# A two-layer encoder trunk on one core: down operands split in place and spread over more products, running sums copied by ScalarE, all down products of layer 0 in chunks, S5 preparation begun beside w_out

## The chip, the cores and the metric

The kernel runs on one core of a Trainium2 chip. The metric is the device time of one execution in microseconds; a kernel's time is the median of its runs.

## The reference

Two pre-norm residual layers over 1024 tokens of width 1024, in float32. Each layer has a token mixer (an S5 state-space branch and a windowed attention branch, gated and summed, then `w_out`) and a SwiGLU feed-forward of width 2816; a final RMSNorm closes. What the change touches is the feed-forward, and the S5 parameters that are prepared beside it:

```python
for layer in range(DEPTH):                      # 2
    hn = rmsnorm(h, norm1_g[layer])
    ...
    h = h + merged @ w_out[layer]
    hn2 = rmsnorm(h, norm2_g[layer])
    ff = jax.nn.silu(hn2 @ ffn_w_gate[layer]) * (hn2 @ ffn_w_up[layer])
    h = h + ff @ ffn_w_down[layer]
```

## The kernel before

All operands are float32, and every product is made of three matmuls of rounded parts (type fp32r): high by high, high by low, low by high. A value is split into parts by a ScalarE cast (the high part) and a VectorE subtraction (the low part); `split` (L113 to L117) does it for activations, L157, L158, L169 and L170 for weights. One matmul multiplies a 128x128 weight tile by a 128x512 operand into one PSUM bank, so the token axis has two halves. `chain` (L181 to L183) makes a whole sum over the contraction in one bank, `piece` (L192 to L194) a part of one.

**The feed-forward** (`ffn_items`, from L1178) has 22 tiles `f` of 128 columns for gate and up. The first `QUAD_FROM` of them (8 on layer 0, 3 on layer 1) are plain: four chains of 24 matmuls. The others are quads: one 2x2 block product by Strassen and Winograd's scheme, gate and up being the two rows and the halves of the tokens the two columns, in seven products of 12 matmuls, 84 instead of 96. A quad's products go into banks x, y, v, w; the sums between them (`first`, `second`, `third`, `gate1`, `half0`: L1400 to L1430) are taken out of PSUM: one ScalarE copy of x, and five VectorE additions per quad. tanh (ScalarE, `ts<-qx`, `ts<-qu`) and two fused VectorE operations per half make the SwiGLU.

**The down products.** On layer 0 the first eight tiles of the feed-forward are multiplied plainly in two groups of four (`GROUPS`); everything else goes in chunks (`CHUNKS`) of eight or six tiles. A chunk's operand is a 2x2 block matrix; seven operand sets (b11, b21, b22 and the sums t0 to t3, formed by VectorE in `row`) are stored to DRAM by POOL's queue (`put`), loaded again by SP's queue (`op_load`, L1225: four tiles of 256 KB a set, tiles `fr`) and split (`op_split`, tiles `foh` and `fol`). `down_quad` then makes two rows of output tiles in seven products again: 16 down quads in all, 33 gate quads. The results of a chunk are added to `hs` in DRAM by accumulating stores on POOL's queue; the last chunk adds into the residual directly, half of it plainly (`last_down`).

**What sets the order.** The program is a list of items; an engine's instructions stand in the order of that list as the tile scheduler then arranges them. `do` counts the products of all quads. `at(t, ...)` hangs work behind product t: for a chunk that begins at product t0, set k is loaded at t0−12+1.7k and split at t0−4+k. `mix` spreads side work over a stretch of items: the operand sums of the first quads over the last 12 plain items, the S5 preparation of layer 1 over the plain items of layer 0. Activation tiles of all kinds share 86 SBUF slots of 128x512 (L44, L107); PSUM has 8 banks; raw weights have four buffers and split weights three, which are fetched and split ahead of their products.

Of the kernel before, what the change touches and what calls it, by code (L numbers as in the profile page):

```python
# [8 lines left out]
F32 = mybir.dt.float32  # L9
F32R = mybir.dt.float32r  # L10
# [15 lines left out]
GROUPS = (((0, 4), (4, 4)), ())  # L26
CHUNKS = (((8, 8), (16, 6)), ((0, 8), (8, 8), (16, 6)))
QUAD_FROM = (8, 3)
DOWN_QUADS = 2
SETS = ("b11", "t1", "t0", "b21", "t2", "t3", "b22")  # L30
# [68 lines left out]
class Trunk:  # L99
# [85 lines left out]
    def piece(self, ps, g, off, xs, start):  # L185

        from functools import partial
        mm = partial(self.nc.tensor.matmul, skip_group_check=not start)
        for k, (xh, xl) in enumerate(xs):
            s = off + k * P  # L190
            wh, wl = g.hi[:, s:s + P], g.lo[:, s:s + P]
            mm(ps, lhsT=wh, rhs=xh, start=start and k == 0, stop=False)  # L192
            mm(ps, lhsT=wh, rhs=xl, start=False, stop=False)  # L193
            mm(ps, lhsT=wl, rhs=xh, start=False, stop=k == len(xs) - 1)  # L194

# [982 lines left out]
    def ffn_items(self, l, fill, head):  # L1178
# [43 lines left out]
        def op_load(c, kind):  # L1222
            ts = ops[c, kind] = [self.A("fr") for _ in range(chunks[c][1] // 2)]
            for j, t in enumerate(ts):
                nc.sync.dma_start(t, fd[c, kind, j])  # L1225

        def op_split(c, kind):
            ops[c, kind] = [self.split(t, "fo") for t in ops[c, kind]]
# [69 lines left out]
        def down_quad(c, m):  # L1298
# [7 lines left out]
            def product(bank, g, off, kind, start):  # L1306
                def run():
                    if start:
# [4 lines left out]
            p = [product(*a) for a in (("x", q.a, 0, "b11", True), ("y", q.b, w, "t1", True), ("v", q.b, 0, "t0", True),  # L1313
                                       ("x", q.a, w, "b21", False), ("y", q.c, 0, "t2", False), ("w", q.d, 0, "t3", True),
                                       ("v", q.e, 0, "b22", False))]
# [7 lines left out]
            def first():  # L1323
                b["p1"] = self.A("qp")
                nc.scalar.copy(b["p1"], b["x"])

            def second():
                b["u2"] = self.A("qu")
                V.tensor_tensor(b["u2"], b["p1"], b["y"], ADD)
# [9 lines left out]
            def third():  # L1339
                V.tensor_tensor(b["p1"], b["p1"], b["y"], ADD)  # L1340
                b["c22"] = self.A("qc")
                V.tensor_tensor(b["c22"], b["p1"], b["v"], ADD)
                out(1, 1, b["c22"])

            def c21():
                V.tensor_tensor(b["p1"], b["p1"], b["w"], ADD)
                out(1, 0, b["p1"])

            def c12():
                V.tensor_tensor(b["u2"], b["u2"], b["v"], ADD)  # L1350
                out(0, 1, b["u2"])
# [28 lines left out]
        def quad_items(f):  # L1380
# [4 lines left out]
            def product(bank, g, off, xs, start):  # L1385
                def run():
# [6 lines left out]
            p = [product("x", q.a, 0, B(0, 0), True), product("y", q.b, HC, lambda: T[1], True),  # L1393
                 product("v", q.b, 0, lambda: T[0], True), product("x", q.a, HC, B(0, 4), False),
                 product("y", q.c, 0, lambda: T[2], False), product("w", q.d, 0, lambda: T[3], True),
                 product("v", q.e, 0, B(1, 4), False)]

            def first():
                b["p1"] = self.A("qp")
                nc.scalar.copy(b["p1"], b["x"])  # L1400

            def second():
                b["u2"] = self.A("qu")
                V.tensor_tensor(b["u2"], b["p1"], b["y"], ADD)
# [5 lines left out]
            def third():  # L1410
                V.tensor_tensor(b["p1"], b["p1"], b["y"], ADD)
                b["c22"] = self.A("qc")
                V.tensor_tensor(b["c22"], b["p1"], b["v"], ADD)

            def half0():
                s = b["s0"]
                V.scalar_tensor_tensor(s, s, 1.0, b["x"], ADD, MUL)
                V.tensor_tensor(b["p1"], b["p1"], b["w"], ADD)
                V.scalar_tensor_tensor(s, b["p1"], 0.5, s, MUL, MUL)  # L1419
                keep(f, 0, s)  # L1420

            def gate1():
                V.tensor_tensor(b["u2"], b["u2"], b["v"], ADD)  # L1423
                b["s1"] = self.A("ts")
                nc.scalar.activation(b["s1"], b["u2"], AF.Tanh, scale=0.5)  # L1425

            def half1():
# [4 lines left out]
                row(f)  # L1432
# [24 lines left out]
        for i, (G, go, U, uo) in enumerate(blocks):  # L1457
# [17 lines left out]
            if i == quads - 1:  # L1475
                w = 12
# [12 lines left out]
        def at(t, fn):  # L1489
            more.setdefault(t, []).append((fn,))  # L1490

        for t0, c in begins:
            for k, kind in enumerate(SETS):
                at(t0 - 12 + k * 17 // 10, lambda c=c, kind=kind: op_load(c, kind))
                at(t0 - 4 + k, lambda c=c, kind=kind: op_split(c, kind))
# [24 lines left out]
        for i, (p, e) in enumerate(made):  # L1520
            do(p[1])
            main.append(e[0])
            do(p[2])
            main.append(e[1])
            do(p[3])
            do(p[4])
            main.append(e[2])
            do(p[5])
            main.append(e[3])
# [3 lines left out]
            main.append(e[4])  # L1533
            do(p[6])
            main.extend(e[5:])
# [9 lines left out]
    def build(self):  # L1545
# [31 lines left out]
        for l in range(DEPTH):  # L1577
# [89 lines left out]
            ffn = self.ffn_items(l, self.s5_prep_items(1) if l == 0 else None, self.w_out_items(l))  # L1667
# [138 lines left out]
```

## Time and profile before

| | |
|---|---|
| median of 3 runs | 2648.95 us (2644.98 to 2649.70) |
| profiled execution, its own time | 2647.83 us |
| its span | 2646.1 us, granted clock 0.986 on the mean |
| TensorE busy | 2564.8 us, 97% |
| VectorE busy | 1827.9 us, 69% |
| ScalarE busy | 1022.1 us, 39% |
| DMA | 357.01 MB, 135 GB/s on the mean |

The profile is of one execution. PE is the engine that multiplies; "idle before, releaser" tells what an engine waited for. The granted clock is the share of full speed at which the throttle let TensorE run. Matmuls overlap in a pipeline: one takes 0.39 us, the next one starts some 0.23 us after it, so the time of a stretch follows from its count of matmuls. The feed-forward of layer 0 ends in the three hundred us from 1186, that of layer 1 in those from 2376.

### The profile page before, as it was taken

To read this page: it belongs to the slowest core of one execution; us is meant where nothing else is said; L and a number is where in the kernel's file an instruction comes from. 1 tells how busy PE (TensorE), PEld (TensorE's weight loads), DVE (VectorE), ACT (ScalarE), POOL (GpSimd) and SP (SyncE) were. 2 spreads that over 40 slices of the span, in tenths; PEclk is the share of its full clock that TensorE was granted. 3 is DMA by queue.
4 is the path that set the end of the run, shared out by engine and by line. 5 is a ranking of instruction groups with operands and counts; after the bars stand their busy time and mean duration, and the time that the engine had idled before them with its cause. 6 is when DMAs were issued, how large, how long until landed. Compare 5 with 4: busy or idle time off the path is not lost.

```text
span 2646.1 us, 35134 instructions
## 1 busy us (share of the span) xinstructions
PE 2564.8 (97%) x12722; PEld 2088.1 (79%) x12722; DVE 1827.9 (69%) x3577; ACT 1022.1 (39%) x1949; POOL 321.3 (12%) x528
## 2 busy tenths in 40 slices
PE   8999899999999999998999999999999999998997
PEld 6787677887888888886787778888878888886776
DVE  9986878575977677677763465756377777676766
ACT  5336744422443333233444553453233222234432
POOL 0141011000142111011100001200001011111110
PEclk9999999999999999998999999999999999998998
DMA  3453435354174533255732244434322233255773
GB/s 139 136 186 118 136 120 180 124 186 140 55 197 132 98 110 108 96 202 137 200 133 76 72 140 161 159 120 167 127 92 93 102 104 116 92 199 156 176 190 123
DMA packets 160510, 357.01 MB, mean 135 GB/s; under 512 B 22048, under 2 KB 44832, under 8 KB 160336
## 3 DMA queue, kind: packets, MB, share of 16 engines
q1 hardware_dynamic: 117136, 236.28, 26.9%
q0 software_dynamic: 43200, 118.48, 15.9%
q8 instruction: 100, 1.64, 0.2%
q14 instruction: 74, 0.61, 0.1%
HBM read 230.97 MB, written 123.68 MB: 134 GB/s over the span
## 4 chain that ended last, share of the span: by engine, by line
PE 88%; DVE 7%; ACT 2%; issue 1%; DMA 1%; SPq 0%; DVEq 0%; ACTq 0%
PE pj L181 6%; PE pj L182 6%; PE pj L183 6%; PE qx L192 3%; PE qx L193 3%; PE qx L194 3%; PE qy L192 3%; PE qy L194 3%; PE qy L193 3%; PE qv L192 3%; PE qv L193 3%; PE qv L194 3%; PE wo L181 2%; PE wo L183 2%; PE wo L182 2%; PE br L181 2%
## 5 line engine op out<-in xcount | busy, mean ns | idle before, releaser
L181 PE MATMUL pj<-rah,whi 128*128 128x512 f32 x768 | 306.2, 399 | 0.4 <-DVE sm L804 0.4
L182 PE MATMUL pj<-ral,whi 128*128 128x512 f32 x768 | 300.1, 391 | 0.7 <-DVE ral L116 0.7
L183 PE MATMUL pj<-rah,wlo 128*128 128x512 f32 x768 | 299.9, 391 | 0.0
L170 DVE TENSOR_TENSOR wlo<-raw,whi 128x1024 fp32r<-128x1024 f32 (+1 forms) x126 | 145.7, 1156 | 168.3 <-ACT whi L169 159.0
L169 ACT CAST whi<-raw 128x1024 fp32r<-128x1024 f32 (+1 forms) x126 | 125.3, 995 | 273.9 <-PE pj L182 115.1
L181 PEld LDWEIGHTS pj<-rah,whi 128*128 128x128 f32 x768 | 144.7, 188 | 35.4 <-issue 4.7
L182 PEld LDWEIGHTS pj<-ral,whi 128*128 128x128 f32 x768 | 144.8, 189 | 30.9 <-DVE ral L116 2.6
L183 PEld LDWEIGHTS pj<-rah,wlo 128*128 128x128 f32 x768 | 144.5, 188 | 30.8
L1425 ACT ACTIVATE ts<-qu 128x512 f32<-128x512 f32 x33 | 20.9, 633 | 287.2 <-DVE qu L1423 287.2
L804 DVE CUSTOM_DVE_ANT_0 x<-s,bias,nsink 128x384 f32<-128x384 f32 (+1 forms) x128 | 67.5, 581 | 64.0 <-PE s L798 63.9
L1423 DVE TENSOR_TENSOR qu<-qu,qv 128x512 f32<-128x512 f32 x33 | 22.7, 687 | 125.8 <-PE qv L194 125.8
L192 PE MATMUL qx<-rfh,whi 128*128 128x512 f32 x264 | 102.7, 389 | 0.0
L193 PE MATMUL qx<-rfl,whi 128*128 128x512 f32 x264 | 102.7, 389 | 0.0
L194 PE MATMUL qx<-rfh,wlo 128*128 128x512 f32 x264 | 102.7, 389 | 0.0
L976 ACT COPY s5sg<-s5s 64x256 f32<-64x256 f32 x128 | 51.7, 404 | 128.8 <-DVE s5s L971 127.4
L181 PE MATMUL wo<-mgh,whi 128*128 128x512 f32 x256 | 100.0, 391 | 0.0
L1196 POOL DMA_DIRECT2D fd_b<-ts x60 | 32.6, 543 | 553.4 <-DVE ts L1419 464.2
L183 PE MATMUL wo<-mgh,wlo 128*128 128x512 f32 x256 | 99.7, 389 | 0.0
L182 PE MATMUL wo<-mgl,whi 128*128 128x512 f32 x256 | 99.6, 389 | 0.0
L157 ACT CAST whs<-s 128x512 fp32r<-128x512 f32 (+1 forms) x98 | 59.9, 612 | 99.3 <-DVE s L150 93.3
L157 ACT CAST whi<-sm 128x1024 fp32r<-128x1024 f32 (+1 forms) x49 | 50.6, 1033 | 122.7 <-PE qv L193 102.9
L158 DVE TENSOR_TENSOR wlo<-sm,whi 128x1024 fp32r<-128x1024 f32 (+1 forms) x49 | 58.9, 1202 | 41.8 <-ACT whi L157 41.7
(468 smaller groups left out, 7191.0 us busy)
## 6 DMA issues: line engine op xcount, KB each, us to landing
raw<-in_w_in SPq DMA_DIRECT2D x52, 512.0 KB
raw<-in_w_gate SPq DMA_DIRECT2D x44, 512.0 KB
raw<-in_w_up SPq DMA_DIRECT2D x44, 512.0 KB
fd_t<-ft POOLq DMA_DIRECT2D x72, 256.0 KB, 2.7
fr<-fd_t SPq DMA_DIRECT2D x72, 256.0 KB
g<-th POOLq DMA_DIRECT2D x64, 256.0 KB, 2.8
thr<-g SPq DMA_DIRECT2D x64, 256.0 KB
fd_b<-ts POOLq DMA_DIRECT2D x60, 256.0 KB, 2.3
```

Of the source, the lines that this page charges most:

```text
L157: nc.scalar.copy(g.hi[:, n], src)
L158: V.tensor_tensor(g.lo[:, n], src, g.hi[:, n].bitcast(F32), SUB)
L169: nc.scalar.copy(g.hi[:, :n], g.raw[:, :n])
L170: nc.vector.tensor_tensor(g.lo[:, :n], g.raw[:, :n], g.hi[:, :n].bitcast(F32), SUB)
L181: mm(ps, lhsT=wh, rhs=xh, start=k == 0, stop=False)
L182: mm(ps, lhsT=wh, rhs=xl, start=False, stop=False)
L183: mm(ps, lhsT=wl, rhs=xh, start=False, stop=k == n - 1)
L192: mm(ps, lhsT=wh, rhs=xh, start=start and k == 0, stop=False)
L193: mm(ps, lhsT=wh, rhs=xl, start=False, stop=False)
L194: mm(ps, lhsT=wl, rhs=xh, start=False, stop=k == len(xs) - 1)
L804: V.tensor_tensor_reduce(out=x[:, :n], in0=ps[:, :n], in1=self.bias[hd][:, bo:bo + n], op0=ADD, op1=ALU.min, scale=-1.0, scalar=self.nsink ...
L976: nc.scalar.copy(SG[64 * r:64 * r + 64, g * 256:(g + 1) * 256].rearrange("p (d n) -> p d n", d=2), Sv[64 * g:64 * g + 64, :, r])
```

## The change

1. Layer 0 has no plain down groups: its chunks are (0,8), (8,8) and (16,6), as on layer 1. One tile more is plain there (`QUAD_FROM` 9), and the sums for the first quads are spread over 20 plain items instead of 12. So 32 gate quads and 20 down quads are left.
2. Operands are loaded into the tile that will hold the low part and split in place: two slots per operand instead of three. The sets come in another order, with loads and splits at times from two tables.
3. `carry`: ScalarE copies the running sum from one PSUM bank to the next (y from x, z and w from y), and the next product adds onto the copy. VectorE is left with two additions per quad (`qc` and `qu`).
4. The first part of the S5 preparation of layer 1 is mixed into the first ten items of `w_out` of layer 0.

The diff, with lines of context left out:

```diff
...
 DEPTH = 2
 NPAIR = 16
 NFF = 22
-GROUPS = (((0, 4), (4, 4)), ())
-CHUNKS = (((8, 8), (16, 6)), ((0, 8), (8, 8), (16, 6)))
-QUAD_FROM = (8, 3)
+GROUPS = ((), ())
+CHUNKS = (((0, 8), (8, 8), (16, 6)), ((0, 8), (8, 8), (16, 6)))
+QUAD_FROM = (9, 3)
+PREP_BEFORE = 40
 DOWN_QUADS = 2
-SETS = ("b11", "t1", "t0", "b21", "t2", "t3", "b22")
+SETS = ("b11", "t0", "t1", "b21", "t2", "b22", "t3")
+LOADS = (-14, -10, -8, -7, -5, -4, -2)
+SPLITS = (-10, -6, -4, -2, 0, 2, 3)
 QUAD_LOOK = 5
 NEG = -1e30
 EPS = 1e-6
...
+    def carry(self, b):
+        nc, V = self.nc, self.nc.vector
+        def first():
+            b["y"] = self.PS("qy")
+            nc.scalar.copy(b["y"], b["x"])
+        def second():
+            b["z"] = self.PS("qz")
+            nc.scalar.copy(b["z"], b["y"])
+            b["sv"] = self.A("qp")
+            nc.scalar.copy(b["sv"], b["v"])
+        def third():
+            b["w"] = self.PS("qw")
+            nc.scalar.copy(b["w"], b["y"])
+            b["c22"] = self.A("qc")
+            V.tensor_tensor(b["c22"], b["sv"], b["y"], ADD)
+        return first, second, third
...
         def op_load(c, kind):
-            ts = ops[c, kind] = [self.A("fr") for _ in range(chunks[c][1] // 2)]
+            ts = ops[c, kind] = [self.A("fol", F32R) for _ in range(chunks[c][1] // 2)]
             for j, t in enumerate(ts):
-                nc.sync.dma_start(t, fd[c, kind, j])
+                nc.sync.dma_start(t.bitcast(F32), fd[c, kind, j])
         def op_split(c, kind):
-            ops[c, kind] = [self.split(t, "fo") for t in ops[c, kind]]
+            pairs = []
+            for lo in ops[c, kind]:
+                hi = self.A("foh", F32R)
+                nc.scalar.copy(hi, lo.bitcast(F32))
+                V.tensor_tensor(lo, lo.bitcast(F32), hi.bitcast(F32), SUB)
+                pairs.append((hi, lo))
+            ops[c, kind] = pairs
...
-            p = [product(*a) for a in (("x", q.a, 0, "b11", True), ("y", q.b, w, "t1", True), ("v", q.b, 0, "t0", True),
-                                       ("x", q.a, w, "b21", False), ("y", q.c, 0, "t2", False), ("w", q.d, 0, "t3", True),
-                                       ("v", q.e, 0, "b22", False))]
+            p = [product(*a) for a in (("x", q.a, 0, "b11", True), ("v", q.b, 0, "t0", True), ("y", q.b, w, "t1", False),
+                                       ("x", q.a, w, "b21", False), ("y", q.c, 0, "t2", False), ("z", q.e, 0, "b22", False),
+                                       ("w", q.d, 0, "t3", False))]
             def out(i, h, x):
                 if at_end:
...
                 else:
                     nc.gpsimd.dma_start(self.hs[m + i, h], x, accum_op=ADD)
-            def first():
-                b["p1"] = self.A("qp")
-                nc.scalar.copy(b["p1"], b["x"])
-            def second():
-                b["u2"] = self.A("qu")
-                V.tensor_tensor(b["u2"], b["p1"], b["y"], ADD)
+            first, second, carry = self.carry(b)
             def c11():
                 if at_end:
...
                 out(0, 0, t)
             def third():
-                V.tensor_tensor(b["p1"], b["p1"], b["y"], ADD)
-                b["c22"] = self.A("qc")
-                V.tensor_tensor(b["c22"], b["p1"], b["v"], ADD)
+                carry()
                 out(1, 1, b["c22"])
             def c21():
-                V.tensor_tensor(b["p1"], b["p1"], b["w"], ADD)
-                out(1, 0, b["p1"])
+                if at_end:
+                    out(1, 0, b["w"])
+                    return
+                t = self.A("dx")
+                nc.scalar.copy(t, b["w"])
+                out(1, 0, t)
             def c12():
-                V.tensor_tensor(b["u2"], b["u2"], b["v"], ADD)
-                out(0, 1, b["u2"])
+                u = self.A("qu")
+                V.tensor_tensor(u, b["sv"], b["z"], ADD)
+                out(0, 1, u)
             return p, [(fn,) for fn in (first, second, c11, third, c21, c12)]
...
                 return (run, g)
             B = lambda h, a: lambda: self.hn2[h][a:a + 4]
-            p = [product("x", q.a, 0, B(0, 0), True), product("y", q.b, HC, lambda: T[1], True),
-                 product("v", q.b, 0, lambda: T[0], True), product("x", q.a, HC, B(0, 4), False),
-                 product("y", q.c, 0, lambda: T[2], False), product("w", q.d, 0, lambda: T[3], True),
-                 product("v", q.e, 0, B(1, 4), False)]
-            def first():
-                b["p1"] = self.A("qp")
-                nc.scalar.copy(b["p1"], b["x"])
-            def second():
-                b["u2"] = self.A("qu")
-                V.tensor_tensor(b["u2"], b["p1"], b["y"], ADD)
+            p = [product("x", q.a, 0, B(0, 0), True), product("v", q.b, 0, lambda: T[0], True),
+                 product("y", q.b, HC, lambda: T[1], False), product("x", q.a, HC, B(0, 4), False),
+                 product("y", q.c, 0, lambda: T[2], False), product("z", q.e, 0, B(1, 4), False),
+                 product("w", q.d, 0, lambda: T[3], False)]
+            first, second, third = self.carry(b)
             def gate0():
                 b["s0"] = self.A("ts")
                 nc.scalar.activation(b["s0"], b["x"], AF.Tanh, scale=0.5)
-            def third():
-                V.tensor_tensor(b["p1"], b["p1"], b["y"], ADD)
-                b["c22"] = self.A("qc")
-                V.tensor_tensor(b["c22"], b["p1"], b["v"], ADD)
             def half0():
                 s = b["s0"]
                 V.scalar_tensor_tensor(s, s, 1.0, b["x"], ADD, MUL)
-                V.tensor_tensor(b["p1"], b["p1"], b["w"], ADD)
-                V.scalar_tensor_tensor(s, b["p1"], 0.5, s, MUL, MUL)
+                V.scalar_tensor_tensor(s, b["w"], 0.5, s, MUL, MUL)
                 keep(f, 0, s)
+                row(f)
             def gate1():
-                V.tensor_tensor(b["u2"], b["u2"], b["v"], ADD)
+                b["u2"] = self.A("qu")
+                V.tensor_tensor(b["u2"], b["sv"], b["z"], ADD)
                 b["s1"] = self.A("ts")
                 nc.scalar.activation(b["s1"], b["u2"], AF.Tanh, scale=0.5)
...
                 V.scalar_tensor_tensor(s, s, 1.0, b["u2"], ADD, MUL)
                 V.scalar_tensor_tensor(s, b["c22"], 0.5, s, MUL, MUL)
                 keep(f, 1, s)
-                row(f)
             return p, [(fn,) for fn in (first, second, gate0, third, half0, gate1, half1)]
...
                 gs = [Granule(self.t["w_down"][l, m, :, f0:f0 + n].rearrange("p k c -> p (k c)"), n * P) for m in range(KT)]
                 downs = [((lambda gi=stops[i], m=m, h=h, g=gs[m]: down(gi, m, h, g)), gs[m]) for m in range(KT) for h in range(2)]
             if i == quads - 1:
-                w = 12
+                w = 12 if early else 20
                 fill_end = len(main) - w
                 downs = self.mix(main[-w:] + downs, extra)
                 del main[-w:]
...
             more.setdefault(t, []).append((fn,))
         for t0, c in begins:
-            for k, kind in enumerate(SETS):
-                at(t0 - 12 + k * 17 // 10, lambda c=c, kind=kind: op_load(c, kind))
-                at(t0 - 4 + k, lambda c=c, kind=kind: op_split(c, kind))
+            for kind, a, b in zip(SETS, LOADS, SPLITS):
+                at(t0 + a, lambda c=c, kind=kind: op_load(c, kind))
+                at(t0 + b, lambda c=c, kind=kind: op_split(c, kind))
         c = len(chunks) - 1
         end = 7 * len(made)
...
         do(made[0][0][0])
         for i, (p, e) in enumerate(made):
+            main.append(e[0])
             do(p[1])
-            main.append(e[0])
             do(p[2])
             main.append(e[1])
             do(p[3])
+            main.append(e[2])
             do(p[4])
-            main.append(e[2])
+            main.append(e[3])
             do(p[5])
-            main.append(e[3])
             if i + 1 < len(made):
                 do(made[i + 1][0][0])
-            main.append(e[4])
+            main.append(e[5])
             do(p[6])
-            main.extend(e[5:])
+            main.extend(e[6:] + [e[4]])
         assert not more, more.keys()
         main += [((lambda m=m, h=h, k=k: last_down(m, h, k, gs[m, k], pst[m])), gs[m, k]) for m, h in plain for k in range(2)]
         if fill:
...
             else:
                 rest = left + [it for p in zip(bb, ba) for it in p]
             self.add(rest)
-            ffn = self.ffn_items(l, self.s5_prep_items(1) if l == 0 else None, self.w_out_items(l))
+            head, fill = self.w_out_items(l), None
+            if l == 0:
+                prep, cost = self.s5_prep_items(1)
+                n = next(i for i in range(len(cost)) if sum(cost[:i]) > PREP_BEFORE)
+                head = self.mix(head[:10], prep[:n], cost[:n]) + head[10:]
+                fill = prep[n:], cost[n:]
+            ffn = self.ffn_items(l, fill, head)
             if l == 0:
                 tail = ffn[-16:]
                 self.add(ffn[:-16])
```

Where the rows of the engines now stand. First ScalarE in an undisturbed gate quad of layer 0 (whi and whs are high parts of wide and narrow weights, ts the tanh, qp a copy in SBUF; qx, qy, qz, qw, qv are PSUM banks). Before:

```order
L157 CAST whi<-sm 128x1024
L157 CAST whi<-raw 128x1024
L157 CAST whs<-s_10960 128x512
L1408 ACTIVATE ts<-qx 128x512
L157 CAST whs<-raw 128x512
L157 CAST whs<-s_10912 128x512
L1425 ACTIVATE ts<-qu 128x512
L1400 COPY qp<-qx 128x512
```

and now:

```order
L206 COPY qy<-qx 128x512
L212 COPY qp<-qv 128x512
L161 CAST whi<-sm 128x1024
L210 COPY qz<-qy 128x512
L161 CAST whi<-raw 128x1024
L1432 ACTIVATE ts<-qx 128x512
L161 CAST whs<-s_10201 128x512
L216 COPY qw<-qy 128x512
L161 CAST whs<-s_10165 128x512
L1445 ACTIVATE ts<-qu 128x512
L161 CAST whs<-raw 128x512
```

The copy of x into SBUF is gone. Four copies stand in its place, three of them into a PSUM bank: z behind a wide weight cast, w behind the tanh of x, y behind the tanh of qu and a narrow cast (the first row shown is this quad's, and the next quad's follows the last row).

Second, ScalarE at the first down chunk of layer 0 (foh is the high part of an operand, fr and fol the tile that was loaded). Before, from the third set on:

```order
L115 CAST foh<-fr 128x512 x4
L1408 ACTIVATE ts<-qx 128x512
L157 CAST whs<-raw 128x512
L115 CAST foh<-fr 128x512 x4
L157 CAST whi<-sm 128x1024
L115 CAST foh<-fr 128x512 x4
L157 CAST whs<-s_11092 128x512
L115 CAST foh<-fr 128x512 x4
L1425 ACTIVATE ts<-qu 128x512
L115 CAST foh<-fr 128x512 x4
L1325 COPY qp<-qx 128x512
L115 CAST foh<-fr 128x512 x4
```

and now, from the first set on:

```order
L1258 CAST foh<-fol 128x512 x4
L216 COPY qw<-qy 128x512
L161 CAST whs<-s_10330 128x512
L206 COPY qy<-qx 128x512
L1445 ACTIVATE ts<-qu 128x512
L161 CAST whs<-raw 128x512
L1258 CAST foh<-fol 128x512 x4
L161 CAST whi<-sm 128x1024
L210 COPY qz<-qy 128x512
L161 CAST whi<-raw 128x1024
L212 COPY qp<-qv 128x512
L1258 CAST foh<-fol 128x512 x4
```

Before, a set of four casts stands after each row or two of the quad's own work; now four or five rows of the quads lie between two sets, and the copies into y, z and w are among them.

## Rows read from the trace of the kernel before

**Rows 1.** The page: busy time of each engine, and the chain that ended last by engine.

```profile
PE 2564.8 (97%) x12722; PEld 2088.1 (79%) x12722; DVE 1827.9 (69%) x3577; ACT 1022.1 (39%) x1949; POOL 321.3 (12%) x528
...
PE 88%; DVE 7%; ACT 2%; issue 1%; DMA 1%; SPq 0%; DVEq 0%; ACTq 0%
```

**Rows 2.** Waits of PE: line waited for, us in total, times, longest.

```profile
PE qw L193 <- DVE fol L116: 14.8, 5, 6.3
PE qw L192 <- ACT foh L115: 13.5, 5, 3.2
...
PE qv L192 <- DVE qc L1413: 5.5, 2, 2.8
...
PE psn L310 <- DVE sqc L301: 2.5, 1, 2.5
PE psn L333 <- DVE rs L91: 2.4, 1, 2.4
...
PE fg L182 <- DVE rfl L116: 2.1, 8, 0.3
...
PE fg L181 <- ACT rfh L115: 1.7, 1, 1.7
```

**Rows 3.** Timeline of PE at layer 0's first chunk: start, us, instruction, idle before and releaser.

```profile
1212.00 0.60 PE L192 MATMUL qw<-foh,whs 128*128 128x512 f32 x1 [2.01 <-ACT foh L115]
...
1218.84 0.79 PE L193 MATMUL qw<-fol,whs 128*128 128x512 f32 x1 [6.24 <-DVE fol L116]
```

**Rows 4.** Stretches, busy us of each engine: five chunk starts and their neighbours.

```profile
core 0: us, PE busy (x) PEld busy (x) DVE busy (x) ACT busy (x) POOL busy (x), PEclk, DMA share, GB/s
1186.00:1225.00 39.00, 27.99 (x107) 21.88 (x106) 33.01 (x52) 21.16 (x37) 3.25 (x6) 0.82 0.38 133
1285.00:1305.00 20.00, 16.19 (x59) 12.46 (x58) 14.26 (x25) 8.63 (x17) 2.58 (x3) 0.83 0.71 181
2046.00:2112.00 66.00, 66.00 (x293) 54.66 (x292) 49.79 (x72) 20.52 (x31) 7.03 (x13) 1.00 0.31 108
2376.00:2415.00 39.00, 27.88 (x105) 21.84 (x105) 34.26 (x54) 20.88 (x37) 3.25 (x6) 0.82 0.33 111
2415.00:2470.00 55.00, 55.00 (x245) 45.54 (x244) 31.70 (x46) 16.05 (x25) 10.30 (x12) 1.00 0.89 227
2445.00:2460.00 15.00, 15.00 (x68) 12.41 (x67) 7.48 (x11) 6.52 (x11) 2.58 (x3) 1.00 1.00 262
2470.00:2495.00 25.00, 20.92 (x85) 16.62 (x84) 22.60 (x37) 16.00 (x30) 3.44 (x4) 0.93 0.54 127
2495.00:2545.00 50.00, 50.00 (x222) 41.42 (x221) 27.55 (x39) 14.04 (x23) 10.32 (x12) 1.00 0.81 194
2545.00:2575.00 30.00, 26.19 (x103) 20.74 (x103) 23.43 (x39) 14.60 (x27) 3.44 (x4) 0.89 0.61 156
```

**Rows 5.** Timeline of DVE in the same place.

```profile
1195.10 2.49 DVE L116 TENSOR_TENSOR fol<-fr,foh 128x512 fp32r<-128x512 f32 x4
```

**Rows 6.** DVE by line: busy us, mean ns, idle before and releaser.

```profile
L1423 DVE TENSOR_TENSOR qu<-qu,qv 128x512 f32<-128x512 f32 x33 | 22.7, 687 | 125.8 <-PE qv L194 125.8
```

**Rows 7.** Timeline of ACT at layer 0's second chunk.

```profile
1295.74 3.21 ACT L115 CAST foh<-fr 128x512 fp32r<-128x512 f32 x6
```

**Rows 8.** ACT by line: busy us, mean ns, idle before and releaser.

```profile
L1425 ACT ACTIVATE ts<-qu 128x512 f32<-128x512 f32 x33 | 20.9, 633 | 287.2 <-DVE qu L1423 287.2
L1400 ACT COPY qp<-qx 128x512 f32<-128x512 f32 x33 | 18.8, 569 | 1.4 <-PE qx L194 1.4
```

**Rows 9.** Timelines of a gate quad of layer 1: PE, then ACT.

```profile
2049.26 0.39 PE L193 MATMUL qv<-tt0l,whi 128*128 128x512 f32 x1
...
2049.74 1.06 ACT L157 CAST whi<-sm 128x1024 fp32r<-128x1024 f32 x1 [3.44 <-PE qv L193]
```

**Rows 10.** Stretches: beside w_out of layer 0, and its plain gate and up products.

```profile
600.00:620.00 20.00, 20.00 (x90) 16.57 (x89) 6.72 (x10) 3.80 (x5) 1.62 (x3) 1.00 0.41 145
700.00:720.00 20.00, 20.00 (x91) 16.61 (x91) 19.28 (x42) 6.80 (x16) 3.67 (x7) 1.00 0.32 79
```

## Prediction

> **What bounds the kernel now.** I read the page's head first: TensorE (PE) is busy 97% of the span and 88% of the chain that ended last; VectorE (DVE) has 7% of that chain and ScalarE (ACT) 2% [rows 1]. So time is won in two ways only: fewer matmuls, or less idle time of PE. The page's totals don't say where PE idles; the table of PE's waits does. Its first two rows are the matmul groups of the down products waiting for their operands' high and low halves, 14.8 and 13.5 us in five waits each; the fifth, 5.5 us, is a sum of the same quads [rows 2]. The timeline of one such place shows one of each kind, 2.01 and 6.24 us [rows 3]. They lie where a chunk of down products begins. There are five such places, and in the table of stretches each shows PE short of its full time and the granted clock below one [rows 4], while the stretches between them are at 1.00.
>
> To price a place I need the pace of PE undisturbed: 66.00 us for 293 matmuls [rows 4], so 0.2253 us each, 2.70 for a product of twelve, 18.93 for a quad of 84. What a place loses is its length less its matmuls at that pace: 39−107×0.2253 = 14.9, 20−59×0.2253 = 6.7, 39−105×0.2253 = 15.3, 25−85×0.2253 = 5.8 and 30−103×0.2253 = 6.8: **49.5 us**, waits and low clock together. The two dear ones are the changes from gate quads to down quads.
>
> Why they are lost is counted on DVE. The splits of a full chunk are 28 subtractions at 0.60 us from start to start (four in 2.49 [rows 5], the last at 0.69), 16.8 us, and the kernel before asks for them within seven products, 18.93 us. A gate quad meanwhile takes 49.79×18.93/66 = 14.3 us of DVE, a down quad 27.55×18.93/50 = 10.4 [rows 4]. That is 31.1 us in 19 at the first kind of place, 12.2 too much (14.9 and 15.3 lost), and 27.2 at the second, 8.3 too much (5.8 to 6.8 lost). The account holds within 3 us, so I trust it for the kernel after.
>
> **The change part by part.**
>
> *Matmuls.* Layer 0 loses 384 plain down matmuls and a gate quad (84), gains a plain gate-and-up tile (96) and four down quads (336): −36, at 0.2253 us **−8.1 us**.
>
> *Operands spread.* The seven sets are split from ten products ahead of the chunk to three behind its start, the last needed six behind it: 16 products, 43.3 us. The sums that leave DVE are three of five in each quad, 0.60 each (one alone 0.687 [rows 6]): 14.3 becomes 12.5 per gate quad, 10.4 becomes 8.6 per down quad. From gate to down: 12.5×10/7 + 8.6×6/7 + 16.8 = 42.1 of 43.3 us, a fit without slack, so a single late set is likely: 1.5 us for each of two places. From down to down: 8.6×16/7 + 16.8 = 36.5 of 43.3, easy on DVE. ScalarE has 20.52×18.93/66 = 5.9 us per quad now [rows 4], three copies more make 7.6, and 28 casts at 3.21/6 = 0.54 us [rows 7] 15.0: 7.6×16/7+15.0 = 32.4 of 43.3. Neither engine explains a stall there any longer. What may is getting the operands in: the DMA share is 0.89 over the stretch ahead of such a place and 1.00 in its worst 15 us [rows 4]. There will be four such places where there were three, since layer 0 gets a third chunk. Bounds: nothing, or today's mean of 6.4 each. The splits begin six products earlier, the loads only two, so I take a third, 2 us each. What stays: 2×1.5+4×2 = **11 us of the 49.5**.
>
> *The Trainium skill on this.* Its page "Perfetto Trace Analysis", under "Identifying Performance Opportunities", says that a gap which repeats on the engine that should be saturated can mean too little SBUF or PSUM for the next tile. By that rule the four places between down chunks keep their gaps, since the tiles still come from 86 slots; it is rival B below. That the two dear gaps fit the count on DVE speaks against it there.
>
> *Copies into PSUM.* 52 quads get a copy y from x, z from y, w from y (ScalarE, PSUM to PSUM), and sv from v. No row shows ScalarE writing PSUM. Nearest are its copy out of PSUM, 569 ns, and its dearest 128x512 row, 633 [rows 8]; I take 0.57. The tight one is z: y's first product, one product of x, and y's second may not start before the copy has read y: 2.70 us. Ahead of it in ScalarE's order stands a weight cast freed by the same product. The same pair is in the trace: the last reader of the weights starts at 2049.26, the product is over a matmul later, 2049.26+2×0.2253 = 2049.71, the cast from 2049.74 for 1.06 [rows 9]. The copy would be done at 2051.4 and is needed at 2052.4: **1.0 us of slack**, cost nothing. Each 0.1 us past that costs 52×0.1 = 5 us. Below nothing it can't go, as PE waits for no sum in a steady quad now. The y copy has 8.1 us from z's end (x, w, v) and stands behind the tanh of qu, the w copy two products and one short cast: hidden, by PE's time.
>
> *First quads of layer 0, S5 preparation.* The sums of the first quads are spread over 20 items instead of 12 and the preparation starts beside w_out, where DVE is busy 6.72 of 20 us and PE 20.00; where it runs now, DVE is at 19.28 of 20 with PE still at 20.00 [rows 10]. So the cover is PE-bound plain products, and it holds for the filler in both places: 0. If the cover were gone, the norm behind w_out would be late: 2.5+2.4 us by the two longest norm waits of today [rows 2]. At best it gives back the 2.1+1.7 us that the first gate products wait now [rows 2].
>
> *Queues.* POOL issues 28 more operand stores and 16 fewer accumulating stores, at 12% busy [rows 1]; SP issues 28 more loads, and those that wait for a slot hold back the weights behind them. Priced with the 2 us per place.
>
> **Sum.** 2647.83 − 8.1 − 49.5 + 11 = 2601.2 for the profiled execution, which is 1.1 below the median of the runs, so **2602 us**.
>
> **The rivals.**
> A, the forecast: 2602. For it: the account above, and in the order of the change each product of the places stands whole, with the splits between them.
> B, operands, not arithmetic, hold the down-to-down places: slots and transfers are as late as today, the four keep 6.4 us each. For it: DMA shares of 0.89 and 1.00 [rows 4]. Against: a split now takes two slots, not three. 2602 − 8 + 25.6 = **2620**.
> C, **slower**: ScalarE's queue works in order, and a copy that PE needs comes too late in every gate quad. The place is the y copy behind the tanh of qu. Today ScalarE stands 287.2/33 = 8.7 us ahead of that tanh [rows 8]. If DVE delivers qu as late as that after z ends, the y copy is ready at 8.7+0.63+0.57 and 0.63 for the narrow cast = 10.5 us, against 8.1: 2.4 us × 32 gate quads = 77, **2679**. It decides from qu 6.3 us late, and eats the whole gain at 1.5 us of delay per gate quad. Against it: the wait of today is for PE's last product of the quad (DVE itself idled 125.8 us ahead of qu for it [rows 6]), and z now ends two products before the quad does. The Trainium skill's page "PSUM — Partial Sum Buffer", under "Engine vs sequencer instructions", states that the queues of ScalarE and VectorE are strict first-in-first-out; no row here shows one overtaking.
> D, the change doesn't do what it says: the splits move, but the stalls stay because the loads behind them come as late as before, and the third chunk start on layer 0 adds one of 6.4: 2647.8 − 8.1 + 6.4 + 1.1 = **2647**. Against: the account fits DVE, which does get relief.
>
> **How the numbers follow.** A 0.68, B 0.21, C 0.07, D 0.04. A change under 0.2%, 5.3 us, can't be told from none here. A and B are both faster: 0.89; D is the same: 0.04; C slower: 0.07. A's own range is 2587 (nothing stays of the 49.5, and the 3.8 us of first gate products come back: 2602−11−3.8) to 2613 (twice the residue). B's goes to 2630: 2620, 5 for the norm, 5 for copies 0.1 us too dear. So the range is 2587 to 2630; C and D are out of it.
>
> **What would show it.** In the profile after: matmul groups qw no longer lead PE's waits, and less than 10 us of waits on operand halves is left; the granted clock at the chunk starts is 0.95 or more; VectorE some 77 us less busy (49×5 sums become 52×2, 28 splits are added: 113 fewer at 0.68); ScalarE's copies into PSUM at 0.5 to 0.7 us. B shows as waits on the cast of the high half whose own releaser is a DMA or a slot, at the second and third chunk of each layer. C shows as PE waiting for L206 or L210 in each quad, evenly over the gate stretch. The prediction is wrong if such a wait appears 30 times, or if waits at the chunk starts stay above 30 us.

## The result, and the profile after

The changed kernel takes **2605.14 us** (2604.28 to 2606.18, 4 runs) against 2649.32 of the kernel before in the same series: ratio of the means 0.9836, 95% interval 0.9819 to 0.9853. The forecast was 2602, the profiled execution 2604.28 (span 2602.5) against a sum of 2601.2. The total is nearly right; two terms in it are not, and they nearly cancel.

The page's first line of engines, against [rows 1]:

```profile
PE 2542.9 (98%) x12686; PEld 2073.4 (80%) x12686; DVE 1759.9 (68%) x3477; ACT 1114.5 (43%) x2109; POOL 323.4 (12%) x540
```
VectorE has 68 us less and ScalarE 92 more. For VectorE 77 were forecast; among what that count left out are the operand sums of the third chunk on layer 0, 16 more of 0.69 us. TensorE's table of waits, against [rows 2] (us in total, times, longest):

```profile
PE psn L336 <- DVE sqb L327: 8.8, 1, 8.8
...
PE qz L197 <- DVE fol L1259: 2.3, 2, 1.2
...
PE qy L196 <- ACT qz L210: 1.5, 2, 0.7
```
The groups `qw` are gone from it; 28.3 us of waits on operand halves have become 2.3, and the copies cost 1.5. New at its head, with 8.8 us, is a wait that [rows 2] does not have: a sum of squares of the norm behind `w_out`. The six chunk starts and the stretch of that norm:

```profile
core 0: us, PE busy (x) PEld busy (x) DVE busy (x) ACT busy (x) POOL busy (x), PEclk, DMA share, GB/s
1120.00:1160.00 40.00, 38.84 (x172) 31.81 (x171) 32.41 (x51) 23.39 (x41) 8.48 (x12) 1.00 0.63 167
1200.00:1240.00 40.00, 40.00 (x178) 33.15 (x177) 28.71 (x44) 23.09 (x40) 8.61 (x10) 1.00 0.74 176
1280.00:1320.00 40.00, 39.26 (x173) 32.18 (x172) 28.04 (x46) 21.74 (x40) 5.73 (x11) 1.00 0.75 242
2360.00:2400.00 40.00, 38.84 (x172) 31.80 (x171) 33.36 (x52) 24.95 (x44) 7.12 (x11) 1.00 0.58 161
2440.00:2480.00 40.00, 40.00 (x179) 33.10 (x177) 30.61 (x46) 23.68 (x41) 8.61 (x10) 1.00 0.74 169
2520.00:2560.00 40.00, 39.26 (x174) 32.14 (x173) 28.87 (x49) 22.53 (x44) 1.19 (x2) 1.00 0.58 175
600.00:640.00 40.00, 35.60 (x158) 29.14 (x156) 33.55 (x78) 11.89 (x27) 10.61 (x18) 1.00 0.56 180
640.00:680.00 40.00, 34.44 (x151) 27.45 (x152) 30.22 (x69) 15.88 (x29) 3.81 (x7) 0.87 0.31 110
```
Four of the starts lose 1.16 or 0.74 us, two lose nothing, and the clock stays at 1.00 in all: 3.8 us for what cost 49.5 [rows 4]. The last two lines have 10.0 us of idle time and, in the second, a clock of 0.87; the kernel before has 2.8 and 1.00 there. Two of the copies into PSUM and the tanh of qu, against [rows 8]:

```profile
L210 ACT COPY qz<-qy 128x512 f32<-128x512 f32 x52 | 30.2, 580 | 2.1 <-PE qy L198 2.1
L206 ACT COPY qy<-qx 128x512 f32<-128x512 f32 x52 | 29.7, 571 | 68.5 <-PE qx L198 68.5
L1445 ACT ACTIVATE ts<-qu 128x512 f32<-128x512 f32 x32 | 20.2, 632 | 72.1 <-DVE qu L1443 72.1
```
A copy into PSUM takes 0.57 to 0.58 us; ScalarE stands 72.1 us ahead of the tanh instead of 287.2. The tight copy of z in a gate quad of layer 1 stands where it was expected:

```profile
2050.81 1.05 ACT L161 CAST whi<-sm 128x1024 fp32r<-128x1024 f32 x1 [1.96 <-PE qy L197]
2051.76 0.58 ACT L210 COPY qz<-qy 128x512 f32<-128x512 f32 x1
2053.48 1.06 ACT L161 CAST whi<-raw 128x1024 fp32r<-128x1024 f32 x1 [1.13 <-PE qx L197]
```
The cast starts as y's product ends, as in [rows 9]; the copy is over at 2052.34, and the next product, of x, ends about 2053.45: 1.1 us of slack, forecast 1.0.

**The new wait.** Four timelines of the changed kernel, of TensorE, SyncE's queue, ScalarE and VectorE:

```profile
644.36 1.87 PE L336 MATMUL psn<-ones,sqb 128*128 128x1 f32 x8 [8.75 <-DVE sqb L327]
```
```profile
618.35 1.85 SPq L1167 DMA_DIRECT2D h<-in_xt  x4
637.79 0.33 SPq L131 DMA_DIRECT2D raw<-in_w_gate  x1
638.16 1.38 SPq L1167 DMA_DIRECT2D h<-in_xt  x3
```
```profile
635.46 1.04 ACT L173 CAST whi<-raw 128x1024 fp32r<-128x1024 f32 x1 [6.87 <-issue]
```
```profile
636.53 1.23 DVE L174 TENSOR_TENSOR wlo<-raw,whi 128x1024 fp32r<-128x1024 f32 x1 [3.44 <-ACT whi L173]
...
642.22 0.69 DVE L1173 TENSOR_TENSOR h<-h,wo 128x512 f32<-128x512 f32 x1 [1.88 <-DMA h<-in_xt]
643.61 0.69 DVE L327 TENSOR_TENSOR sqb<-sqb,sq 128x512 f32<-128x512 f32 x1 [0.70 <-ACT sq L326]
```
In SyncE's queue a weight load (637.79) stands behind four residual loads. It needs a raw buffer; that is free when VectorE has made the low part of the weights in it (636.53 to 637.76), which follows the cast at 635.46. That cast starts 0.25 us behind the start of TensorE's last `wo` matmul ahead of the wait (635.21), so it is read as waiting for a weight buffer that TensorE held, though its own row names no releaser. The three residual loads behind the weight load go at 638.16, the residual's sum is made at 642.22 and its squares at 643.61. Mixing the preparation into `w_out` had put those three loads behind that weight load: without it (experiment 7) four residual loads go at 616.95, and only the last one stands behind the weight load of 639.29.

### The profile page after: what moved, and what is told of

Same layout as the page of the kernel before. It is cut to its first block, busy times and chain, and to the rows that moved or that the text cites. A ratio compares the mean times of both kernels' runs of the same rounds, so it can differ in the third digit from the quotient of the medians.

```text
span 2602.5 us, 35115 instructions
## 1 busy us (share of the span) xinstructions
PE 2542.9 (98%) x12686; PEld 2073.4 (80%) x12686; DVE 1759.9 (68%) x3477; ACT 1114.5 (43%) x2109; POOL 323.4 (12%) x540
## 4 chain that ended last, share of the span: by engine, by line
PE 89%; DVE 6%; ACT 2%; issue 1%; DMA 1%; SPq 0%; DVEq 0%; ACTq 0%
PE pj L185 7%; PE pj L186 6%; PE pj L187 6%; PE qx L197 3%; PE qx L198 3%; PE qy L196 3%; PE qx L196 3%; PE qy L197 3%; PE qy L198 3%; PE br L185 2%; PE br L186 2%; PE br L187 2%; PE wo L185 2%; PE wo L186 2%; PE wo L187 2%; PE qz L197 2%
## 5 line engine op out<-in xcount | busy, mean ns | idle before, releaser
L174 DVE TENSOR_TENSOR wlo<-raw,whi 128x1024 fp32r<-128x1024 f32 x112 | 137.1, 1224 | 160.8 <-ACT whi L173 151.4
L173 ACT CAST whi<-raw 128x1024 fp32r<-128x1024 f32 x112 | 117.3, 1049 | 249.8 <-PE pj L186 114.9
L1222 POOL DMA_DIRECT2D fd_b<-ts x72 | 39.3, 546 | 660.6 <-DVE ts L1450 318.7
L1259 DVE TENSOR_TENSOR fol<-fol,foh 128x512 fp32r<-128x512 f32 x160 | 100.2, 686 | 15.8 <-ACT foh L1258 15.8
L212 ACT COPY qp<-qv 128x512 f32<-128x512 f32 x52 | 30.5, 586 | 158.6 <-PE qv L198 153.7
L1258 ACT CAST foh<-fol 128x512 fp32r<-128x512 f32 x160 | 88.0, 618 | 0.0
```

Source lines behind the costliest of these rows:

```text
L173: nc.scalar.copy(g.hi[:, :n], g.raw[:, :n])
L174: nc.vector.tensor_tensor(g.lo[:, :n], g.raw[:, :n], g.hi[:, :n].bitcast(F32), SUB)
L1258: nc.scalar.copy(hi, lo.bitcast(F32))
L1259: V.tensor_tensor(lo, lo.bitcast(F32), hi.bitcast(F32), SUB)
```

## The experiments

Where nothing else is said, each is the changed kernel with one edit, timed beside the kernel before, which took 2647.80 to 2647.90 us there. The changed kernel has its time from another series (2649.32 for the kernel before), so a difference from it of some 1.5 us means nothing. The edits are shown in short. The parts are named: matmuls (chunks, one plain tile more, 20 items), spread (the two tables of times), in place, carry, preparation.

**1. Without the spread.**

```diff
-at(t0 + a, load); at(t0 + b, split)
+at(t0 - 12 + k * 17 // 10, load); at(t0 - 4 + k, split)
```

> All of the change except the two tables of times: sets are loaded and split at the old times (within seven products), in the new order. Theory 1 (the stalls at the chunk starts were VectorE's backlog of splits): 16.8 us of splits and 12.5 us of a gate quad in 18.9 us are 10.4 us too much at each of two places, 16.8 and 8.6 in 18.9 are 6.5 too much at each of four, so some 47 us come back against the 3 that the change leaves: 2645 to 2650, with waits of TensorE on the halves of the operands first in the table. Theory 2 (the copies by ScalarE and two slots per operand were enough): under 2615.

2605.86 us, ratio 0.9840 [0.9825, 0.9855]: no difference. Theory 1 falls. ScalarE's casts at the first chunk, and TensorE there:

```profile
1110.45 1.66 ACT L1255 CAST foh<-fol 128x512 fp32r<-128x512 f32 x3
...
1138.77 4.26 ACT L1255 CAST foh<-fol 128x512 fp32r<-128x512 f32 x8
```
```profile
1135.22 0.50 PE L193 MATMUL qy<-foh,whs 128*128 128x512 f32 x1 [0.81 <-ACT qz L207]
```
The first operand matmul starts at 1120.65. Casts run from 10.2 us ahead of it to 22.4 behind it, 32.6 us, and TensorE waits 0.81. The old times never asked for the splits within seven products: the last set is needed only eight products after the first.

**2. Without the carry**: the old sums, products and order of sets.

```diff
-y <- x, z <- y, w <- y, sv <- v on ScalarE; matmuls add onto the copies
+p1 <- x on ScalarE; u2, p1, c22, p1, u2 by five VectorE additions
```

> All of the change except the copies by ScalarE: the sums are five VectorE additions per quad again, with the old order of the products, the new times and the operands in place. Theory 1: a gate quad takes 14.3 us of VectorE and a down quad 10.4, so from gate to down 46.1 us of work stand against 43.3, 2.8 us late at two places, and 40.6 against 43.3 at the other four: 2608 to 2614. Theory 2 (the sums in VectorE's queue held the operands back as much as the splits' times did): 2625 or more, with waits at all six places.

2618.37 us, 0.9887 [0.9870, 0.9903]: 13.2 more than the change, between the two theories, at two places only, where gate quads end. TensorE, ScalarE and VectorE there:

```profile
1133.48 0.50 PE L195 MATMUL qx<-foh,whi 128*128 128x512 f32 x1 [1.69 <-ACT qp L1335]
...
1140.83 0.79 PE L195 MATMUL qy<-foh,whs 128*128 128x512 f32 x1 [4.31 <-DVE qu L1339]
```
```profile
1132.33 0.63 ACT L1435 ACTIVATE ts<-qu 128x512 f32<-128x512 f32 x1 [2.06 <-DVE qu L1433]
1132.86 0.57 ACT L1335 COPY qp<-qx 128x512 f32<-128x512 f32 x1
```
```profile
1131.61 0.69 DVE L1433 TENSOR_TENSOR qu<-qu,qv 128x512 f32<-128x512 f32 x1 [0.63 <-PE qv L197]
...
1137.68 2.49 DVE L1236 TENSOR_TENSOR fol<-fol,foh 128x512 fp32r<-128x512 f32 x4
1140.09 0.68 DVE L1339 TENSOR_TENSOR qu<-qp,qy 128x512 f32<-128x512 f32 x1
```
This is a ring, read upwards: y's second product (1140.83) waits for the sum `qu<-qp,qy`, which has to read y first; that sum stands behind four splits (1137.68) and other work, with no gap in VectorE's rows since 1131.61; x's second product (1133.48) waited for the copy of x (1132.86), which stands behind the tanh (1132.33), which waits for the sum of 1131.61, and that one for TensorE's own product v. So Theory 3 was formed for what follows: what counts is which work TensorE waits for, and what stands ahead of it in order.

**3. Three more VectorE additions per quad that nothing reads**, with the new and the old times.

```diff
+V.tensor_tensor(self.A("qj"), b["sv"], b["sv"], ADD)   # one in second, two in third
```

> All of the change, and in each quad VectorE makes three additions more of 128x512 from SBUF that nothing reads: its amount of work is that of five sums again, but TensorE waits for none of the three. Theory 1 (amount of VectorE's work): the places where gate quads end lose what they lose with five real sums, 2613 to 2620. Theory 3 (what TensorE waits for, not how much VectorE does): 2604 to 2608.

> The same three additions per quad, with the old times of loads and splits (compare: the change with the old times). Theory 1: the account of the prediction, 31.1 us of VectorE's work in 18.9, applies in full and the stalls return: 2630 or more. Theory 3: the copies keep TensorE free of VectorE's queue except for the halves: 2604 to 2612. In between, both count.

2609.40 us, 0.9856 [0.9841, 0.9871], and 2617.31, 0.9886 [0.9869, 0.9902]: both lie between the windows of the two theories, so both count. First lines of TensorE's waits at the chunks, new times, then old:

```profile
PE qy L196 <- ACT qz L210: 4.7, 6, 0.8
```
```profile
PE qy L193 <- ACT qz L207: 8.6, 4, 2.8
```
With the new times, VectorE's amount costs 4.3 us at most (the three results take slots, too), a third of the 13.2; the rest of the carry's worth is what TensorE no longer waits for. With the old times the same amount costs 7.9 more, 12.2 in all, against the 49.5 that the kernel before lost at its starts [rows 4] with these times and five real sums (and three slots per operand). So the spread is worth something only where VectorE has more to do than the carry leaves it.

**4. The copies on VectorE.**

```diff
-nc.scalar.copy(b["z"], b["y"])   # y, w alike
+V.tensor_copy(b["z"], b["y"])
```

> All of the change, but the copies y from x, z from y, w from y are made by VectorE; ScalarE keeps the one of v. Theory 3 (the ring through VectorE's queue): TensorE waits for a VectorE copy in many quads, most at the chunk starts, 2625 or more. Theory 1 (amount): VectorE has 1.8 us more per quad, as with five sums, and the new times leave room for that: 2608 to 2614.

2615.25 us, 0.9877 [0.9860, 0.9893]: just above Theory 1's window and well below Theory 3's. TensorE waits 4.0 us at each of the two gate-to-down places, for high halves, and 1.2 us in all for copies. Theory 3 was too strong: in steady quads VectorE's queue serves TensorE in time. The order of products is that of the change, and yet 10.1 of the 13.2 us are lost again; so it is not that order by itself that the carry is worth. And VectorE is busy for 1850.4 us here as in experiment 3 with the new times, yet this kernel is 5.9 us slower: amount is not all. The casts that TensorE waits for stand behind a weight cast that itself waited 1.49 us for TensorE's product x; why they stand there is open.

**5. Three slots per operand**: tiles `fr` are loaded and split into two new ones.

> All of the change except the split in place: a third slot per operand while it is split. If slots never ran short: 2603 to 2608. Rival B of the prediction (slots and transfers hold the starts of the chunks): 2612 to 2625, with loads that wait for a release and TensorE waiting on high halves at the second and third chunks.

2616.96 us, 0.9884 [0.9869, 0.9899]: 11.8 more. ScalarE and TensorE at layer 0's first chunk:

```profile
1114.60 1.06 ACT L160 CAST whi<-raw 128x1024 fp32r<-128x1024 f32 x1
1115.56 0.61 ACT L118 CAST foh<-fr 128x512 fp32r<-128x512 f32 x1
...
1135.62 2.17 ACT L118 CAST foh<-fr 128x512 fp32r<-128x512 f32 x4
```
```profile
1136.29 0.79 PE L195 MATMUL qy<-foh,whs 128*128 128x512 f32 x1 [2.47 <-ACT foh L118]
```
The casts of one set now stand singly between the quad's own work, as those of the first set did in the kernel before, and a later set's stand behind a weight cast, the tanh and a narrow cast; TensorE waits 2.47 us for it. The slots matter, as rival B said, but mostly where gate quads end (3.2 and 3.6 us of idle time), little at the second chunks (1.3 each) and not at the third. That the scheduler ordered the casts so because it saw no free slots is argued, not shown.

**6. Single parts on the kernel before.**

> The kernel before with the copies by ScalarE (and the order of products and sets that goes with them) and nothing else: old chunks, old times, three slots per operand. Theory 3 (what stalled TensorE was not VectorE's amount of work but a ring: a product waits for a sum, the sum stands behind a weight's low part in VectorE's queue, that one waits for its high part, whose buffer a product of TensorE holds; the copies take the sums out of the ring): the five places lose under 6 us together, 2600 to 2608. Theory 2 (two slots per operand are needed as well): 2615 to 2635. Theory 1 (amount of VectorE's work at the old times): 2640 or more.

> The kernel before with operands split in place and the new times, nothing else: five VectorE sums per quad, old chunks. Theory 3: the ring stays where gate quads end (6 us at each of two places, as with all but the copies), and the down-to-down places are free: 2610 to 2616. If the spread alone is worth nothing: 2640 or more.

> The kernel before with all down products of layer 0 in chunks, one plain tile more, and the sums of the first quads over 20 items; no other part. 36 matmuls less are 8.1 us, a third chunk start on layer 0 costs 6 to 7: 2644 to 2649, with waits of TensorE on operand halves at six places. If the plain down products were a better cover for something (the preparation, the sums), 2650 or more.

Carry alone: 2612.81, 0.9867 [0.9853, 0.9882]. Spread and in place: 2615.69, 0.9879 [0.9864, 0.9894]. Matmuls alone: 2653.94, 1.0022 [1.0013, 1.0031], 6.0 us longer than the kernel before, where 2644 to 2649 was expected, or 2650 and more if the plain down products were a better cover for something. Carry alone misses Theory 3's window by 5 us and lies between it and Theory 2's: its five places lose 7.3 us of idle time. Spread and in place lies where Theory 3 had it. Carry alone gives 35 us, spread and in place 32, and the whole change 44: they remove the same stalls, so their worths do not add. What each leaves is what the part that it lacks was worth above. The change without its matmuls and its cost at the norm would stand at 2605.1+8.1−9.5 (experiment 8) = 2603.7: carry alone stands 9 above that and has three slots (11.8 in experiment 5), the other stands 12 above it and has the old sums (13.2 in experiment 2). The waits of matmuls alone, and 120 us of it, then of the kernel before (columns as above):

```profile
PE qw L192 <- ACT foh L115: 16.5, 6, 3.2
PE qw L193 <- DVE fol L116: 16.0, 6, 6.3
PE fg L181 <- ACT rfh L115: 7.3, 3, 6.3
```
```profile
600.00:720.00 120.00, 111.59 (x493) 89.36 (x492) 89.51 (x234) 38.47 (x75) 14.73 (x26) 0.97 0.32 103
```
```profile
600.00:720.00 120.00, 117.19 (x527) 95.34 (x526) 87.32 (x225) 38.91 (x72) 8.54 (x16) 1.00 0.28 90
```
Six waits instead of five on each half, against [rows 2], and first gate products that wait 7.3 us in place of 1.7, with a lower clock behind them. Priced as in the prediction, by matmuls at the undisturbed pace, the norm and the first gate products lose 34×0.2253 = 7.7 us here, and 1.3 more as `w_out` began that much earlier (558.5 against 559.8): 9.0. In stretches of 50 us the three starts of layer 0 lose 13.5, 5.8 and 6.7, the two of the kernel before 15.1 and 7.0: 3.9 more. So −8.1+9.0+3.9 = +4.8. From the first `wo` matmul of layer 0 to that of layer 1 the two traces show +5.5 (1309.3 against 1303.8), with 6362 matmuls for 6398: the sum closes within 1 us, so 36 matmuls less are worth about their 8.1 us, and the lost cover takes them back.

**7. Preparation not moved**, and **8. residual loads four items ahead**, with and without the move.

```diff
-x = self.h2[m, h] = self.A("h2"); nc.sync.dma_start(x, src[m, h])
+for a in order[len(loads):order.index((m, h)) + 1 + 4]:   # layer 0 only
+    x = self.h2[a] = self.A("h2"); nc.sync.dma_start(x, src[a]); loads.append(a)
```

> All of the change except the preparation of layer 1 beside w_out: it runs beside the plain products of layer 0 again. Theory 1 (the 8.75 us that TensorE now waits for the norm's squares behind w_out come from that move): the wait goes and the time falls to 2593 to 2598. Theory 2 (the plain products of layer 0, now nine tiles without plain down products, have too little cover for the preparation and the sums of the first quads): the wait goes, but TensorE waits for those sums or the preparation ends late, 2605 or more.

> All of the change, and in layer 0 each item of w_out issues the loads of the residual for the next four items. Theory 1 (the 8.75 us wait is one of SyncE's queue: three residual loads stood behind a weight load that waited for its buffer until TensorE had finished the items before): the wait falls under 2 us, the granted clock there stays at 1, 2593 to 2597. Theory 2 (VectorE beside w_out has too much to do with the preparation): the wait stays above 5 us, 2601 to 2605.

> Residual loads four items ahead, and the preparation not moved (compare: residual loads ahead alone). If the move of the preparation is worth something once its cost in SyncE's queue is gone, the 6.4 us wait of the first gate products for high halves that stand behind the preparation's copies in ScalarE's queue stays: 2600 to 2605. If the move is worth nothing: 2594 to 2598.

Not moved: 2603.48, 0.9832 [0.9817, 0.9846], between the windows of its two theories. The 8.8 us are gone, and another wait is there, on ScalarE:

```profile
PE fg L183 <- ACT rfh L117: 7.3, 3, 6.4
```
```profile
669.74 0.43 ACT L547 COPY PB<-pr 128x128 f32<-128x128 f32 x1 [3.06 <-DVE pr L496]
...
671.75 0.61 ACT L117 CAST rfh<-y 128x512 fp32r<-128x512 f32 x1
```
The preparation's copies stand ahead of the casts of the norm's result and wait 3.06 us for VectorE themselves. Loads ahead: **2595.62, 0.9802 [0.9787, 0.9816]**, faster than both kernels; SyncE's queue there:

```profile
599.50 1.82 SPq L1170 DMA_DIRECT2D h<-in_xt  x4
...
624.65 0.91 SPq L1170 DMA_DIRECT2D h<-in_xt  x2
640.56 0.33 SPq L132 DMA_DIRECT2D raw<-in_w_gate  x1
```
All residual loads are out by 625.6, ahead of the weight load of 640.56, and TensorE has 40.00 of the 40 us from 600 on and 38.64 of the next 40, where its clock is 0.96. Loads ahead without the move: 2604.17, 0.9835 [0.9820, 0.9849], where the wait on `rfh` stays, 6.8 us. So the move is worth 8.5 us once its price in SyncE's queue (9.5 us) is not paid; in the change as it is the two nearly cancel.

## Why the prediction was right, and where it was not

- **What bounds the kernel, and matmuls.** Right: TensorE's idle time at the chunk starts was the gain. The −8.1 holds within 1 us (experiment 6), but the matmuls' part alone comes with a third start and less cover behind the norm, and is slower.
- **"What stays: 11 us of the 49.5."** 3.8 us stayed. Gate to down: 1.16 twice, forecast 1.5. Down to down: 0, 0, 0.74 and 0.74, forecast 2 each; the share of the DMA engines, 0.82 to 0.87 in the 40 us ahead of these starts and 0.58 to 0.75 at them, did not hold them.
- **"The account holds within 3 us, so I trust it."** The step that failed as a cause. Seven products were the times at which the program hangs up the splits, not the span in which they are needed; for the kernel after, the prediction itself counted 16 products up to the one that needs the last set, so like was not set against like. Over four products of the gate kind and eight of the down kind (12×2.70 = 32.4 us) the kernel before had 14.3×4/7+10.4×8/7+16.8 = 36.9 us of VectorE's work, 4.5 too much, and lost 15. The agreement was chance. [rows 4] had a sign of it: VectorE, said to be 12.2 us short at the first place, is busy there for 33.01 of 39 us. The rest of the loss is in the main queue order, as experiments 2 and 3 show, and the trace of the kernel before has the ring itself at that place:

```profile
1202.42 1.04 ACT L157 CAST whi<-sm 128x1024 fp32r<-128x1024 f32 x1 [2.79 <-PE qv L193]
...
1203.49 1.22 DVE L158 TENSOR_TENSOR wlo<-sm,whi 128x1024 fp32r<-128x1024 f32 x1 [2.29 <-ACT whi L157]
1204.63 0.68 DVE L1413 TENSOR_TENSOR qc<-qp,qv 128x512 f32<-128x512 f32 x1
...
1205.37 0.78 PE L192 MATMUL qv<-rfh,whs 128*128 128x512 f32 x1 [2.77 <-DVE qc L1413]
...
1210.03 0.69 DVE L1423 TENSOR_TENSOR qu<-qu,qv 128x512 f32<-128x512 f32 x1 [1.71 <-PE qv L194]
...
1210.81 0.63 ACT L1425 ACTIVATE ts<-qu 128x512 f32<-128x512 f32 x1 [2.66 <-DVE qu L1423]
```

TensorE waits 2.77 us for the sum qc, which stands behind a weight's low part, for whose high part VectorE itself stood idle 2.29 us, and ScalarE's cast of it was released by TensorE's product v. Then VectorE waits for TensorE's last product of the gate quad and the tanh for VectorE; behind the tanh stand the casts that TensorE waits for at 1212.00 [rows 3]. Only the last wait, 6.24 us for a split of 1218.10, is one in which VectorE has no gap: that split stands behind six operations of the gate quad, 3.9 us.
- **Spread.** Credited with the gain; worth nothing beside the carry (experiment 1), 7.9 us with more work on VectorE.
- **Copies.** Right: 0.57 us, 1.1 us of slack. Where it ran out, 0.74 us was lost, in each last chunk, whose products have nine matmuls.
- **"So the cover is PE-bound plain products: 0."** The mis-sized term: 9.5 us, twice the bound of 4.9. I had priced VectorE's cover, which was there, and named SyncE's queue the wrong way round: residual loads were held back by a weight load. 2601.2 − 7.2 + 9.5 = 2603.5, measured 2604.28: that the total came out so near is partly luck.
- **Rivals.** B's places were nearly free, though its slots matter (experiment 5). C did not happen to the copies; its mechanism is seen in experiment 2, a copy behind the tanh behind a sum (1132.33 and 1132.86). That agrees with the strict order of the queues that the Trainium skill's page "PSUM — Partial Sum Buffer" states under "Engine vs sequencer instructions". The rule of the Trainium skill's page "Perfetto Trace Analysis", under "Identifying Performance Opportunities", on repeated gaps did not hold at the four places it was used for (0 to 0.74 us lost), and is consistent with experiment 5, 11.8 us for a third slot. D's picture, stalls that stay and one start more, is what the matmuls' part shows alone.

Open: why the scheduler sets the casts apart when operands take three slots, and why the awaited casts come late when VectorE makes the copies.

## What to carry to other kernels

Before an account of work against time is believed, check over which span the results are due, and whether the suspected engine is ever idle there; that the account matches a loss is not proof. One kernel that gives the suspected engine more work, which nothing reads, tells amount from order. When work is moved, list what is issued on each queue behind each waiting entry of it: here three loads behind one weight load cost about as much as the move gave. Parts that remove the same stall should not be summed.

## What was not expected of the hardware

ScalarE copies 128x512 from PSUM to PSUM in 571 to 580 ns, about as long as from PSUM to SBUF (586 ns for `qp<-qv` of the changed kernel, 569 [rows 8]).
